# Expert 0 as a narrow block that shares the stretch of place 2; weight loads and stages in pairs

## The chip, the cores and the metric

One NeuronCore of a Trainium2 chip runs the whole kernel. The metric is the device time of one execution in microseconds. The kernel before was timed in three runs, and one more execution was profiled.

## The reference, cut to what matters

The kernel computes a two-layer decoder trunk on 256 tokens of 1024 features in fp32: a recurrent mixer and a dense SwiGLU, then a differential attention and a mixture of eight experts, of which each token takes two. The change lies in the mixture of experts:

```python
logits = xt @ w_router                       # 256 tokens x 8 experts
top_v, top_e = lax.top_k(logits, 2)
gates = softmax(top_v)
# per expert e, for the tokens x that chose it:
gu = x @ w13[e]                              # 1024 -> 2 * 3584
y  = (silu(gu[:, :3584]) * gu[:, 3584:]) @ w2[e]
out[token] += gate * y
```

Each expert's weights are 3 x 1024 x 3584 fp32 numbers, 44 MB. With the reference's inputs the experts 0 to 7 are chosen by 36, 21, 66, 43, 130, 105, 85 and 26 tokens.

## The kernel before, in words

**Numbers as pairs.** Every fp32 operand is split in a high part of type fp32r (ScalarE copies it) and a low remainder (VectorE subtracts). A product is then three matmuls on TensorE: high x high, low x high, high x low (`mm3`, lines 306 to 309). Tokens are the stationary operand (128 x 128), weights the moving one (128 x 512).

**Stream** (lines 35 to 89) brings the weights: `load` issues 1 MB loads on SyncE's queue as long as a slot is free, `split` makes a set of each half of a load (ScalarE line 77, VectorE line 78) as long as one of five pairs of parts is free, and `take` hands a set to TensorE. So the split runs at most five sets ahead of TensorE. Slots are four `raw`, the two `x_hi` and `x_lo`, `h1` (`h` in the profile), four `early` ones (`e`) and, once each, `h3_hi` and `h3_lo`. The `early` slots go round until `retire` takes them back in expert 3, where a pool named `mt` gets their memory.

**Places and blocks.** Expert 0 is at place 0; the experts 1 to 7 are sorted by their number of tokens, and take the places 1 to 7. `plan` works the order, the ranks and the gates out on VectorE and GpSimd, step by step beside the first sets. A place has blocks of 128 tokens (wide) or 64 (narrow). Place 1 has a wide and a narrow block, 0 and 2 to 4 have a wide one, 5 to 7 a narrow one. In a wide block a set costs six matmuls of 512 columns. A narrow block holds the high parts of its tokens in 64 columns of the stationary operand and the low parts in the other 64, so a set costs four (lines 1186 and 1187), and the two halves of the result are added by four small matmuls with `fold`, two stacked unit matrices (line 1207), where a wide block has four transposes (line 1197).

**Stages.** A place has seven chunks of 512 hidden columns; each has a stage g (gate half), u (other half) and w (back to 1024 features), of four sets each. `stages` orders them g0 u0 g1 u1 w0 g2 u2 w1 and so on. `moe_seq` is 0, then 2, then 3, then place 1 with the narrow places 7, 6, 5 mixed in by `merge`, then 4. After each set `beat_` takes a step of `quick` (the sums or transposes of the last chunk) and at every second set one of `slow` (plan, gathers, results). If more tokens than a place holds chose an expert, a branch behind the stages (`more`) would run another block.

Of the kernel before, what the change touches and what calls it, by code (L numbers as in the profile page):

```python
# [19 lines left out]
T = 256  # L20
D = 1024
# [13 lines left out]
class Stream:  # L35


    def __init__(self, nc, free, room):

        self.nc, self.free, self.room = nc, deque(free), deque(room)  # L40
        self.todo, self.loaded, self.ready, self.hold, self.retired = deque(), deque(), deque(), False, ()

    def add(self, ap, a, b, cols=False):
        self.todo.append((ap, a, b, cols))

    def add_plain(self, dst, src):

        self.todo.append((src, dst, None, None))

    def load(self):  # L50
        while self.todo and (self.todo[0][2] is None or self.free):
            ap, a, b, cols = self.todo.popleft()
            if b is None:
                self.nc.sync.dma_start(a, ap)
                continue
# [37 lines left out]
def trunk(ctx, tc, x, mem, a_w_in, a_conv_w, a_conv_b, a_w_rgate, a_b_rgate, a_w_igate, a_b_igate,  # L93
# [56 lines left out]
    PLACE = {0: [(0, 0, 128)], 1: [(1, 0, 128), (1, 128, 64)], 5: [(5, 0, 64)], 6: [(6, 0, 64)], 7: [(7, 0, 64)]}  # L150
# [4 lines left out]
    def stages(p):  # L155
        for j in range(NJ + 1):
            if j < NJ:
                yield (p, "g", j)
                yield (p, "u", j)
            if j:  # L160
                yield (p, "w", j - 1)

    def chain(*places):

        out_ = []
        for p in places:
            s_ = list(stages(p))
            out_ = out_[:-1] + s_[:2] + out_[-1:] + s_[2:] if out_ else s_
        return out_
# [17 lines left out]
    assert moe_seq[-5] == (4, "w", NJ - 3)  # L187
    moe_seq.insert(-2, moe_seq.pop(-5))
# [8 lines left out]
    def stage_loads(seq):  # L197
        def rows_(w, p, r0, nk, c0, n):
            if p == 0:
                return wslice(w[0, 0], r0, nk, c0, n)  # L200
            return lambda: w[0, ds(expert_id(p), 1), r0:r0 + nk * 128, c0:c0 + n].rearrange(
                "o (k p) f -> p (o k) f", p=128)

        for p, kind, j in seq:
            for k in range(2):
                if (p, kind, j, k) == (4, "w", NJ - 1, 1):

                    for r in range(2):
                        yield rows_(moe_w2, p, j * 512 + k * 256 + r * 128, 1, 0, D), 1, D
                elif kind == "w":  # L210
                    yield rows_(moe_w2, p, j * 512 + k * 256, 2, 0, D), 2, D
                else:
                    yield rows_(moe_w13, p, k * 512, 4, j * 512 + (FFN if kind == "u" else 0), 512), 4, 512
# [707 lines left out]
    for item in stage_loads(moe_seq):  # L921
        st.add(*item)
# [37 lines left out]
    def mt():  # L960

        if "mt" not in late:
            assert not any(slot in early for _, slot in st.loaded) and not any(slot in early for slot in st.free)
# [8 lines left out]
    early = [(rp, f"e{i}", True) for i in range(N_EARLY)]  # L972
# [38 lines left out]
    GROUP = ([(0, 0, 128)], [(1, 0, 128)], [(1, 128, 64), (7, 0, 64)], [(6, 0, 64), (5, 0, 64)],  # L1011
# [10 lines left out]
    dispatch((0, 0, 128), val)  # L1022
# [3 lines left out]
    fold = mo.tile([128, 64], F32, name="fold")  # L1026
    y = h3
# [3 lines left out]
    def plan():  # L1031
# [25 lines left out]
        POOL.tensor_copy(ord_i, ordr[0:1])  # L1057
        yield
# [43 lines left out]
        POOL.tensor_add(fold, ident[:, 0:64], ident[:, 64:128])  # L1102
# [10 lines left out]
    class Block:  # L1113
        def __init__(self, b):
# [3 lines left out]
            self.bank = int(self.place in (5, 6, 7))  # L1118
            self.h, self.ready = {}, False

# [10 lines left out]
    def beat_():  # L1131
        beat[0] += 1
        step(quick)
        if beat[0] % 2:
            step(slow)

    def gather_first(b):

        b.x = [mw.tile([128, KT, 128], F32R, name=f"xg_{s}") for s in ("hi", "lo")]
        for k0, n in ((0, 2), (2, 2), (4, 4)):  # L1140
            p = bank()[:, :n * 128].rearrange("p (k c) -> p k c", k=n)
            for k in range(n):
# [45 lines left out]

    def hidden(b, j):

        yield
        if b.wide:
            yield
            yield
            p = bank().rearrange("p (i c) -> p i c", i=4)
            for i in range(4):
                PE.transpose(p[:, i], b.sg[:, i * 128:(i + 1) * 128], ident)  # L1197
            hd = [mt().tile([128, 4, 128], F32R, name="hs", bufs=4) if (b.place, j) == (4, NJ - 1) else
                  mw.tile([128, 4, 128], F32R, name=f"hd_{s}") for s in ("hi", "lo")]
            hi, lo = hd  # L1200
        else:
            h = mt().tile([128, 4, 64], F32, name="sh")
            for src in (b.gs, b.us):

                p = bank()[:, :256].rearrange("p (i c) -> p i c", i=4)
# [267 lines left out]
```

## Time and profile before

| | us |
|---|---|
| median of 3 runs | 1606.11 |
| lowest and highest | 1605.93, 1607.49 |
| the profiled execution | 1606.54 |
| its span, from first to last instruction | 1604.8 |
| TensorE busy | 1582.8 (99%) |
| VectorE busy | 1263.1 (79%) |
| ScalarE busy | 1091.9 (68%) |

The span misses 1.7 us of the execution's time. The mixture of experts begins at 572 us with the first sets of expert 0, and its last stage ends at 1588 us. A busy share is an average over the whole span; the matmuls' ends are modelled, so two matmuls that follow each other overlap in the records, and their price is read from start to start.

### The profile page before, as it was taken

How to read it: one execution, taken by the hardware profiler on the slowest of the kernel's cores; microseconds unless marked ns; L12 is line 12 of the kernel's file. 1: busy time of each engine (PE TensorE's matmuls, PEld its weight loads, DVE VectorE, ACT ScalarE, POOL GpSimd, SP SyncE). 2: the span in 40 equal slices, each digit the busy share in tenths (PEclk: the TensorE clock that was granted, in tenths of full speed). 3: DMA queues.
4: the chain of work that ended last, by engine and by line, in shares of the span. 5: the costliest groups of instructions: out<-in, count | busy, mean ns of one | idle time of the engine just before them, and what ended most of it. 6: DMA issues, size and time to landing. Idle time of an engine off the chain costs nothing.

```text
span 1604.8 us, 23215 instructions
## 1 busy us (share of the span) xinstructions
PE 1582.8 (99%) x8585; PEld 1340.6 (84%) x8585; DVE 1263.1 (79%) x1464; ACT 1091.9 (68%) x1419; POOL 37.1 (2%) x60
## 2 busy tenths in 40 slices
PE   8999999999999999999999999999999999999996
PEld 7988999998998877888888888888888888888775
DVE  6678545546657689888988879888798889789976
ACT  5784544443546368787787778778778777778774
POOL 0000000000000113000000000000000000000000
PEclk9999999999999999999999999999999999999998
DMA  9454655556443789999996999999999999999991
GB/s 290 158 190 151 237 185 185 184 187 205 135 133 135 272 302 352 356 357 332 360 364 224 352 309 341 355 357 370 326 354 359 362 365 345 336 362 359 342 321 47
DMA packets 218682, 451.63 MB, mean 281 GB/s; under 512 B 7241, under 2 KB 62610, under 8 KB 218562
## 3 DMA queue, kind: packets, MB, share of 16 engines
q1 hardware_dynamic: 217490, 446.76, 78.5%
q0 software_dynamic: 1072, 3.32, 0.7%
q8 instruction: 69, 1.13, 0.3%
q14 instruction: 51, 0.42, 0.1%
HBM read 449.00 MB, written 1.05 MB: 280 GB/s over the span
## 4 chain that ended last, share of the span: by engine, by line
PE 93%; DVE 3%; ACT 2%; issue 1%; DMA 1%; POOL 0%; POOLq 0%; SPq 0%; ACTq 0%
PE mm L307 14%; PE mm L309 14%; PE mm L308 14%; PE mm L1186 7%; PE mm L1187 7%; PE acc L307 7%; PE acc L308 7%; PE acc L309 7%; PE mm L1207 3%; PE acc L1186 3%; PE acc L1187 2%; DVE w_lo L78 2%; PE mm L1170 1%; PE mm L1197 1%; ACT w_hi L77 1%
## 5 line engine op out<-in xcount | busy, mean ns | idle before, releaser
L78 DVE TENSOR_TENSOR w_lo<-raw,w_hi 128x1024 fp32r<-128x1024 f32 x509 | 610.1, 1223 | 188.3 <-ACT w_hi L77 184.8
L77 ACT ACTIVATE w_hi<-raw 128x1024 fp32r<-128x1024 f32 x509 | 525.3, 1056 | 141.4 <-PE mm L308 42.8
L307 PE MATMUL mm<-w_hi,xg_hi 128*128 128x512 f32 x560 | 225.2, 402 | 0.2 <-ACT w_hi L77 0.2
L307 PE MATMUL mm<-x_hi,w_hi 128*128 128x256 f32 x768 | 220.4, 287 | 2.4 <-ACT w_hi L77 2.4
L308 PE MATMUL mm<-w_lo,xg_hi 128*128 128x512 f32 x560 | 221.4, 395 | 1.2 <-DVE w_lo L78 1.2
L309 PE MATMUL mm<-w_hi,xg_lo 128*128 128x512 f32 x560 | 221.3, 395 | 0.0
L309 PE MATMUL mm<-x_hi,w_lo 128*128 128x256 f32 x768 | 218.6, 285 | 1.1 <-DVE w_lo L78 1.1
L308 PE MATMUL mm<-x_lo,w_hi 128*128 128x256 f32 x768 | 218.0, 284 | 0.0
L1186 PE MATMUL mm<-w_hi,xs 128*128 128x512 f32 x448 | 179.0, 400 | 0.0
L1187 PE MATMUL mm<-w_lo,xs 128*128 128x512 f32 x448 | 176.9, 395 | 0.0
L307 PEld LDWEIGHTS mm<-x_hi,w_hi 128*128 128x128 f32 x768 | 148.0, 193 | 5.6 <-ACT w_hi L77 2.9
L309 PEld LDWEIGHTS mm<-x_hi,w_lo 128*128 128x128 f32 x768 | 148.0, 193 | 1.7 <-DVE w_lo L78 1.6
L308 PEld LDWEIGHTS mm<-x_lo,w_hi 128*128 128x128 f32 x768 | 148.0, 193 | 0.6
L307 PEld LDWEIGHTS mm<-w_hi,xg_hi 128*128 128x128 f32 x560 | 105.3, 188 | 25.7 <-ACT xs L1352 1.5
L309 PEld LDWEIGHTS mm<-w_hi,xg_lo 128*128 128x128 f32 x560 | 105.1, 188 | 25.2
L308 PEld LDWEIGHTS mm<-w_lo,xg_hi 128*128 128x128 f32 x560 | 105.4, 188 | 24.9 <-DVE w_lo L78 2.2
L78 DVE TENSOR_TENSOR w_lo<-x_hi,w_hi 128x1024 fp32r<-128x1024 f32 x86 | 103.7, 1223 | 15.3 <-ACT w_hi L77 15.2
L78 DVE TENSOR_TENSOR w_lo<-x_lo,w_hi 128x1024 fp32r<-128x1024 f32 x86 | 103.4, 1222 | 13.4 <-ACT w_hi L77 13.2
L78 DVE TENSOR_TENSOR w_lo<-h,w_hi 128x1024 fp32r<-128x1024 f32 x84 | 100.9, 1222 | 14.4 <-ACT w_hi L77 14.0
L307 PE MATMUL acc<-w_hi,hd_hi 128*128 128x512 f32 x272 | 108.1, 398 | 0.0
L308 PE MATMUL acc<-w_lo,hd_hi 128*128 128x512 f32 x272 | 107.4, 395 | 0.0
L309 PE MATMUL acc<-w_hi,hd_lo 128*128 128x512 f32 x272 | 107.4, 395 | 0.0
(379 smaller groups left out, 2645.6 us busy)
## 6 DMA issues: line engine op xcount, KB each, us to landing
raw<-in_moe_w SPq DMA_DIRECT2D x169, 1024.0 KB, 5.5
x_hi<-in_moe_w SPq DMA_DIRECT2D x43, 1024.0 KB, 5.4
x_lo<-in_moe_w SPq DMA_DIRECT2D x43, 1024.0 KB, 6.2
raw<-in_ffn_w SPq DMA_DIRECT2D x42, 1024.0 KB, 5.0
h<-in_moe_w SPq DMA_DIRECT2D x42, 1024.0 KB, 5.5
e<-in_moe_w SPq DMA_DIRECT2D x36, 1024.0 KB, 5.9
raw<-in_a_w_in SPq DMA_DIRECT2D x10, 1024.0 KB, 9.5
raw<-in_mem_w_kv SPq DMA_DIRECT2D x8, 1024.0 KB
```

Of the source, the lines that this page charges most:

```text
L77: nc.scalar.activation(hi, src, AF.Copy)
L78: nc.vector.tensor_sub(lo, src, hi.bitcast(F32))
L307: PE.matmul(o, lhsT=l_hi, rhs=r_hi, start=start, stop=False)
L308: PE.matmul(o, lhsT=l_hi, rhs=r_lo, start=False, stop=False)
L309: PE.matmul(o, lhsT=l_lo, rhs=r_hi, start=False, stop=stop)
L1170: PE.matmul(p[:, k], lhsT=src[:, t, f], rhs=disp[:, t, g0:g0 + ng], start=t == 0, stop=t == 1)
L1186: PE.matmul(o[h], lhsT=w[:, kt], rhs=w_hi[:, i, f], start=a, stop=False)
L1187: PE.matmul(o[h], lhsT=w[:, kt], rhs=w_lo[:, i, f], start=False, stop=z)
L1197: PE.transpose(p[:, i], b.sg[:, i * 128:(i + 1) * 128], ident)
L1207: PE.matmul(p[:, i], lhsT=src[:, i * 128:(i + 1) * 128], rhs=fold, start=True, stop=True)
```

## The change

**Places.** Expert 0 becomes a narrow block of 64 tokens. It runs its first four runs alone (`head`), the rest is mixed by `merge` with place 2, which starts at its ninth stage.

**Stages in pairs.** `stages` now gives lists of two stages: g0 g1, u0 u1, g2 g3, w0 w1, u2 u3, and so on; `merge` and `join` move such runs as a whole.

**Loads.** For a pair of g or u stages four loads of 2 x 128 rows and 1024 columns (4 KB pieces of a row instead of 2 KB) come together: the first halves of all four feed the first stage, the second halves the second, so each of the four slots is held until the second stage is split. A load for w takes two neighbouring rows per partition (8 KB instead of 2 x 4 KB); so that the sums still meet, `rows_of` takes every second hidden column when the chunk is transposed or folded. The `early` slots are used once. The first loads of other experts wait in `Stream.load` until `plan` has made the order known (`known`).

**Sums.** `turn_half` folds the g half and the u half apart, each three sets behind its copy out of the accumulator. While the head runs, `slow` steps at every set, and the gather of place 2 follows `plan` at once. The rows of the last norm (`late_rows`) use other buffers, and the branch for too many tokens covers more cases.

```diff
-    PLACE = {0: [(0, 0, 128)], 1: [(1, 0, 128), (1, 128, 64)], ...
+    PLACE = {0: [(0, 0, 64)], 1: [(1, 0, 128), (1, 128, 64)], ...
     def stages(p):
-        for j in range(NJ + 1):
-            if j < NJ:
-                yield (p, "g", j)
-                yield (p, "u", j)
-            if j:
-                yield (p, "w", j - 1)
+        runs = [range(j, min(j + 2, NJ)) for j in range(0, NJ, 2)]
+        for n, js in enumerate(runs):
+            yield [(p, "g", j) for j in js]
+            if n:
+                yield [(p, "w", j) for j in runs[n - 1]]
+            yield [(p, "u", j) for j in js]
+        yield [(p, "w", j) for j in runs[-1]]
...
-        return a[:-1] + b[:2] + a[-1:] + b[2:]
-    moe_seq = join(chain(0, 2, 3), merge(chain(1), chain(7, 6, 5)))
+        return a[:-1] + b[:1] + a[-1:] + b[1:]
+    head = 4
+    moe_seq = chain(0)[:head] + merge(chain(2), chain(0)[head:])
+    moe_seq = join(join(moe_seq, chain(3)), merge(chain(1), chain(7, 6, 5)))
...
+    def add_all(self, loads, cols=False):
+        loads = [(self.n + i, *load, cols) for i, load in enumerate(loads)]
+        self.n += len(loads)
+        self.todo += loads
+        for h in range(2 if loads[0][2] > 1 else 1):
+            self.cuts += [(load[0], h) for load in loads]
...
     def load(self):
-        while self.todo and (self.todo[0][2] is None or self.free):
+        while self.todo and (self.todo[0][0] is None or self.free):
+            if callable(self.todo[0][1]) and not self.known:
+                return
...
     def split(self):
-            halves, slot = self.loaded[0]
-            src = halves.pop(0)
-            if not halves:
-                self.loaded.popleft()
-                if slot[2] and slot not in self.retired:
+            n, h = self.cuts.popleft()
+            halves, slot = self.loaded[n]
+            src = halves[h]
+            if h == len(halves) - 1:
+                del self.loaded[n]
+                if slot[2]:
                     self.free.append(slot)
...
             if kind == "w":
+                        a = rows_(moe_w2, p, j * 512 + k * 256, 2, 0, D, "(p k)")
...
+                if len(run) == 2:
+                    yield [(rows_(moe_w13, p, k * 256, 2, c0, 1024), 2, 1024) for k in range(4)], True
...
-    early = [(rp, f"e{i}", True) for i in range(N_EARLY)]
+    early = [(rp, f"e{i}", False) for i in range(N_EARLY)]
...
-        if beat[0] % 2:
+        if beat[0] % 2 or beat[0] < 8 * head:
             step(slow)
...
+    def rows_of(a, i):
+        n = i // 2 * 256 + i % 2
+        return a[:, n:n + 255:2]
+
+    def turn_half(b, j, a, u):
+        yield
+        yield
+        yield
+        p = bank()[:, :256].rearrange("p (i c) -> p i c", i=4)
+        for i in range(4):
+            PE.matmul(p[:, i], lhsT=rows_of(a, i), rhs=fold, start=True, stop=True)
+        if not u:
+            b.sh[j] = b.room([128, 4, 64], F32, "sh")
+            ACT.activation(b.sh[j], p, AF.Silu)
+            return
+        h = b.sh.pop(j)
+        DVE.tensor_mul(h, h, p)
+        yield
+        hd = b.room([128, 4, 128], F32R, "hs")
+        hi, lo = hd[:, :, 0:64], hd[:, :, 64:]
+        ACT.activation(hi, h, AF.Copy)
+        DVE.tensor_sub(lo, h, hi.bitcast(F32))
+        b.h[j] = hd
...
-        (0, "u", 3): [ask(4, True, blocks[2])],
-        (3, "g", 2): [retire],
...
-    slow.append(plan())
+    slow += [plan(), gather(4, True, blocks[2])]
```

On TensorE, the first products behind expert 0's gather. Before, each weight row block takes three matmuls on the wide block `xg`:

```order
L307 MATMUL mm<-w_hi,xg_hi 128x512
L308 MATMUL mm<-w_lo,xg_hi 128x512
L309 MATMUL mm<-w_hi,xg_lo 128x512
L307 MATMUL mm<-w_hi,xg_hi 128x512
L308 MATMUL mm<-w_lo,xg_hi 128x512
L309 MATMUL mm<-w_hi,xg_lo 128x512
```

and now two on the narrow block, which lies in the buffer `ys`:

```order
L1231 MATMUL mm<-w_hi,ys_5635 128x512
L1232 MATMUL mm<-w_lo,ys_5635 128x512
L1231 MATMUL mm<-w_hi,ys_5635 128x512
L1232 MATMUL mm<-w_lo,ys_5635 128x512
```

One set is the six rows of the first and the four of the second piece.

On VectorE, the plan's steps for the gates among the splits of expert 0's weights (`w_lo`). The reduction to `gate` reads products that GpSimd makes from the result of the reciprocal. Before:

```order
L1072 RECIPROCAL g_5939<-g_5939 128x2
L78 TENSOR_TENSOR w_lo<-e_5590,w_hi 128x1024
L1216 TENSOR_TENSOR hd_lo<-mm,hd_hi 128x512
L78 TENSOR_TENSOR w_lo<-e_5592,w_hi 128x1024 x2
L78 TENSOR_TENSOR w_lo<-x_hi,w_hi 128x1024
L1083 TENSOR_REDUCE gate<-tmp 128x2x7
L78 TENSOR_TENSOR w_lo<-x_hi,w_hi 128x1024
L78 TENSOR_TENSOR w_lo<-x_lo,w_hi 128x1024
L1088 TENSOR_REDUCE cs<-cmp 128x7
```

and now:

```order
L1108 RECIPROCAL g_5820<-g_5820 128x2
L95 TENSOR_TENSOR w_lo<-h_hi,w_hi 128x1024
L95 TENSOR_TENSOR w_lo<-h_lo,w_hi 128x1024
L1119 TENSOR_REDUCE gate<-tmp 128x2x7
L95 TENSOR_TENSOR w_lo<-h_5584,w_hi 128x1024
L1124 TENSOR_REDUCE cs<-cmp 128x7
L95 TENSOR_TENSOR w_lo<-e_5586,w_hi 128x1024
L1131 TENSOR_REDUCE over<-cs 128x1
```

Between the reciprocal and the reduction stood four splits and a remainder; now two splits stand there.

On SyncE, the queue of loads where the static ones of expert 0 end. Before (the rows before these are the first twelve loads of the mixture):

```order
L59 DMA e_5592<-in_moe_w 128x4x512
L59 DMA x_hi<-in_moe_w 128x4x512
L59 DMA x_lo<-in_moe_w 128x2x1024
L59 DMA raw<-in_moe_w 128x2x1024
```

and now, at the same place, with the read of the experts' order (`TENSOR_LOAD`) behind 16 loads:

```order
L71 DMA e_5592<-in_moe_w 128x2048
L71 DMA x_hi<-in_moe_w 128x2048
L71 DMA x_lo<-in_moe_w 128x2048
L71 DMA raw<-in_moe_w 128x2048
L213 TENSOR_LOAD ord_i
L71 ISA
L71 DMA raw<-in_moe_w 128x2x1024
```

The 16 loads before the read feed the head; place 2's first load stands right behind it, and its pieces are twice as long.

## Rows read from the trace of the kernel before

**Rows 1.** The page: busy time, share of the span and instructions of each engine; and the chain that ended last, by engine.
```profile
PE 1582.8 (99%) x8585; PEld 1340.6 (84%) x8585; DVE 1263.1 (79%) x1464; ACT 1091.9 (68%) x1419; POOL 37.1 (2%) x60
PE 93%; DVE 3%; ACT 2%; issue 1%; DMA 1%; POOL 0%; POOLq 0%; SPq 0%; ACTq 0%
```

**Rows 2.** The longest waits of TensorE's matmuls (PE) and of its weight loads (PEld) from 572 to 1588 us: who waited for whom, us in total, times, longest.
```profile
PE mm L308 <- DVE w_lo L78: 1.2, 2, 0.8
PEld mm L308 <- DVE w_lo L78: 2.2, 3, 1.1
```

**Rows 3.** Three windows: length, then busy us and number of instructions of PE, PEld, DVE, ACT and POOL, the granted TensorE clock, the share of the transfer engines and GB/s.
```profile
600.00:860.00 260.00, 259.56 (x1184) 210.83 (x1183) 234.57 (x230) 206.23 (x233) 12.25 (x21) 1.00 0.98 353
1020.00:1140.00 120.00, 120.00 (x592) 99.66 (x592) 104.52 (x104) 94.26 (x118) 0.00 (x0) 1.00 1.00 363
1400.00:1520.00 120.00, 120.00 (x567) 97.62 (x567) 113.79 (x118) 95.52 (x114) 2.09 (x4) 1.00 0.98 355
```

**Rows 4.** Timeline of TensorE: start, length, instruction, number of records. The first row is expert 0's first matmul, that of 819.59 expert 3's first. From 660.02 to 665.62 there are 24 matmuls from start to start. L1170 are gather products, L1197 transposes, L1207 folds (four of them in eight records).
```profile
572.41 0.48 PE L307 MATMUL mm<-w_hi,xg_hi 128*128 128x512 f32 x1
...
630.47 0.39 PE L309 MATMUL mm<-w_hi,xg_lo 128*128 128x512 f32 x1
630.70 0.56 PE L1170 MATMUL mm<-disp,h_hi 128*128 128x128 f32 x4
...
631.38 0.39 PE L308 MATMUL mm<-w_lo,xg_hi 128*128 128x512 f32 x1
...
660.02 0.40 PE L309 MATMUL mm<-w_hi,xg_lo 128*128 128x512 f32 x1
...
665.62 0.40 PE L309 MATMUL mm<-w_hi,xg_lo 128*128 128x512 f32 x1
...
709.89 0.40 PE L309 MATMUL acc<-w_hi,hd_lo 128*128 128x512 f32 x1
710.12 0.60 PE L1197 MATMUL mm<-ident,sg 128*128 128x128 f32 x4
...
710.79 0.39 PE L308 MATMUL mm<-w_lo,xg_hi 128*128 128x512 f32 x1
...
819.59 0.48 PE L307 MATMUL mm<-w_hi,xg_hi 128*128 128x512 f32 x1
...
1280.07 0.39 PE L1187 MATMUL acc<-w_lo,hs 128*128 128x512 f32 x1
1280.30 1.00 PE L1207 MATMUL mm<-fold,gs 128*128 128x64 f32 x8
...
1281.43 0.40 PE L1187 MATMUL acc<-w_lo,hs 128*128 128x512 f32 x1
```

**Rows 5.** Timeline of VectorE from expert 0's first sets on; in brackets idle time before the instruction and what ended it. The split at 574.27 is the first after the gather, the one at 616.36 the 31st.
```profile
574.27 1.23 DVE L78 TENSOR_TENSOR w_lo<-x_hi,w_hi 128x1024 fp32r<-128x1024 f32 x1 [0.25 <-ACT w_hi L77]
...
588.01 0.68 DVE L1303 TENSOR_TENSOR sg<-sg,mm 128x512 f32<-128x512 f32 x1
...
594.03 0.68 DVE L1216 TENSOR_TENSOR hd_lo<-mm,hd_hi 128x512 fp32r<-128x512 f32 x1
...
605.33 0.15 DVE L1072 RECIPROCAL g<-g 128x2 f32<-128x2 f32 x1
605.41 1.21 DVE L78 TENSOR_TENSOR w_lo<-e,w_hi 128x1024 fp32r<-128x1024 f32 x1
606.53 0.68 DVE L1216 TENSOR_TENSOR hd_lo<-mm,hd_hi 128x512 fp32r<-128x512 f32 x1
607.13 2.35 DVE L78 TENSOR_TENSOR w_lo<-e,w_hi 128x1024 fp32r<-128x1024 f32 x2
609.40 1.22 DVE L78 TENSOR_TENSOR w_lo<-x_hi,w_hi 128x1024 fp32r<-128x1024 f32 x1
611.43 0.26 DVE L1083 TENSOR_REDUCE gate<-tmp 128x14 f32<-128x98 f32 x1 [0.81 <-POOL tmp L1082]
...
616.36 1.21 DVE L78 TENSOR_TENSOR w_lo<-raw,w_hi 128x1024 fp32r<-128x1024 f32 x1
...
621.63 1.22 DVE L1107 TENSOR_TENSOR h_lo<-h,h_hi 128x1024 fp32r<-128x1024 f32 x1
...
630.17 4.62 DVE L78 TENSOR_TENSOR w_lo<-e,w_hi 128x1024 fp32r<-128x1024 f32 x4
```

**Rows 6.** Groups of instructions by line: the product and the remainder of a narrow block's hidden columns on VectorE; busy us in total, mean ns of one, idle time before.
```profile
L1216 DVE TENSOR_TENSOR hs<-sh,hs 128x256 fp32r<-128x256 f32 x28 | 11.8, 421 | 0.0
L1211 DVE TENSOR_TENSOR sh<-sh,mm 128x256 f32<-128x256 f32 x28 | 11.7, 416 | 0.0
```

**Rows 7.** Timeline of GpSimd (POOL) between that reciprocal and that reduction.
```profile
605.57 1.09 POOL L1073 TENSOR_TENSOR d<-d,g 128x2 f32<-128x2 f32 x1 [15.66 <-DVE g L1072]
...
607.08 3.61 POOL L1078 TENSOR_TENSOR ge<-ge,c 128x16 f32<-128x16 f32 x1
...
610.89 0.50 POOL L1082 TENSOR_TENSOR tmp<-sel,ge 128x49 f32<-128x49 f32 x2
```

**Rows 8.** SyncE's transfer queue in two windows, first from 180 to 430 us, then from 600 to 860 us: packets, MB, and the time that they took as a share of 16 engines' time.
```profile
q1 hardware_dynamic: 33995, 45.36, 54.2%
...
q1 hardware_dynamic: 38388, 91.50, 98.0%
```

**Rows 9.** The page: transfers by slot and tensor, number, KB each, median us from issue to landing.
```profile
raw<-in_moe_w SPq DMA_DIRECT2D x169, 1024.0 KB, 5.5
```

More of the change, by code (lines that the diff above doesn't have):

```diff
@@ L166, in chain @@
         for p in places:
[L167 to L168 removed]
+            out_ = join(out_, list(stages(p)))
         return out_
@@ L962, in mt @@
         if "mt" not in late:
-            assert not any(slot in early for _, slot in st.loaded) and not any(slot in early for slot in st.free)
+            assert not st.uses(early)
             ep.close()
@@ L1117, in __init__, with room @@
             self.wide = self.n == 128
-            self.bank = int(self.place in (5, 6, 7))
+            self.bank = int(self.place in (0, 5, 6, 7))
             self.h, self.ready = {}, False
+            self.sg, self.sh = {}, {}
+        def room(self, shape, dtype, name):
+            if "mt" in late or not st.uses(early):
+                pool, bufs = mt(), {"xs": 3, "gu": 3, "sh": 4, "hs": 4}[name]
+            else:
+                pool, bufs = mw, 2
+                name = {"xs": "ys0", "gu": "sg", "sh": "hd_hi", "hs": "hd_lo"}[name]
+            return pool.tile(shape, dtype, name=name, bufs=1 if name == "ys0" else bufs)
     quick, slow, beat = deque(), deque(), [0]
@@ L1189, in hidden @@
     def hidden(b, j):
         yield
[L1192 to L1205, printed above, removed]
-                for i in range(4):
-                    PE.matmul(p[:, i], lhsT=src[:, i * 128:(i + 1) * 128], rhs=fold, start=True, stop=True)
-                if src is b.gs:
-                    ACT.activation(h, p, AF.Silu)
-                else:
-                    DVE.tensor_mul(h, h, p)
-                yield
-            hd = mt().tile([128, 4, 128], F32R, name="hs", bufs=4)
-            hi, lo, p = hd[:, :, 0:64], hd[:, :, 64:], h
+        yield
@@ L1215, in hidden @@
+        yield
+        p = bank().rearrange("p (i c) -> p i c", i=4)
+        for i in range(4):
+            PE.transpose(p[:, i], rows_of(b.sg[j], i), ident)
+        del b.sg[j]
+        hd = [mt().tile([128, 4, 128], F32R, name="hs", bufs=4) if (b.place, j) == (4, NJ - 1) else
+              mw.tile([128, 4, 128], F32R, name=f"hd_{s}") for s in ("hi", "lo")]
+        hi, lo = hd
         ACT.activation(hi, p, AF.Copy)
@@ L1347, in spread @@
             gb.extend(mt().tile([128, D], F32, name="xs", bufs=3) for _ in range(2))
[L1348 removed]
+            for i in range(4):
                 p = bank()
[L1350 removed]
+                f = slice(i % 2 * 512, (i % 2 + 1) * 512)
+                PE.matmul(p, lhsT=slots[0:1, 1:2].to_broadcast([1, 128]), rhs=rows[i // 2][:, f], start=True, stop=True)
                 yield
[L1352 removed]
+                ACT.activation(gb[i // 2][:, f], p, AF.Copy)
         slow.append(spread())
[L1356 to L1360 removed]
     hooks = {
[L1363 removed]
         (2, "g", 0): [gathered(*blocks[2])],
@@ L1386, in trunk @@
     with tc.If(more > 0):
-        for p in (0, 1, 2, 3, 5, 6, 7):
+        rooms = {p: sum(b[2] for b in bs) for p, bs in PLACE.items()}
+        most = {p: T if p < 2 else 2 * T // p for p in PLACE}
+        for p, base in ((p, base) for p in PLACE for base in range(rooms[p], most[p], 128)):
             c = nc.values_load(cs_i[0:1, p:p + 1], min_val=0, max_val=2 * T,
                                skip_runtime_bounds_check_because="a count of at most 256 tokens")
-            with tc.If(c > 0):
-                key = (p, sum(b[2] for b in PLACE[p]), 128)
+            with tc.If(c > base - rooms[p]):
+                key = (p, base, 128)
                 where[key] = (0, 0)
@@ L1400, in trunk @@
                 s2 = stream()
+                s2.known = True
                 for item in stage_loads(seq):
-                    s2.add(*item)
-                for p_, kind, j in seq:
-                    run_stage([b], kind, j, s2)
+                    s2.add_all(*item)
+                for run in seq:
+                    for _, kind, j in run:
+                        run_stage([b], kind, j, s2)
                 wait_slow()
     fs = [slice(h * 512, (h + 1) * 512) for h in range(2)]
-    ys = [mt().tile([128, 512], F32, name=n) for n in ("gs", "us")]
+    ys = [mt().tile([128, 512], F32, name="gu", bufs=3) for _ in range(2)]
     ACT.activation(ys[0], last.acc[0], AF.Copy)
```

114 lines of the change are left out of this document (57 added, 57 removed).

## The prediction

> **What bounds the kernel now.** I read the page first: TensorE (PE) is busy for 99% of the span and makes up 93% of the chain that ended last [rows 1]. A busy PE can still be a waiting PE, so the waits come next: between 572 and 1588 us, the whole mixture of experts, PE waited 1.2 us for the low half of a weight and its weight loads 2.2 us for the same thing [rows 2]. The windows show how little the others have left: from 600 to 860 us VectorE (DVE) is busy for 234.6 of 260 us and the transfers for 0.98 of the time; both stay near there to the end [rows 3]. So three resources are nearly full, and PE is the one that sets the end. The timeline gives its prices [rows 4]: 24 matmuls of 512 columns start within 665.62 - 660.02 = 5.60 us, 0.2333 us each, with the granted clock at 1.00 throughout, the 2.4 GHz level [rows 3]. A set (half a load) is 6 of them for a wide block, 1.40 us, and 4 for a narrow one, 0.93 us. DVE splits a set in (4.62 - 1.22)/3 = 1.135 us when sets follow each other [rows 5]: less than a wide set, more than a narrow one.
>
> **Expert 0 narrow: PE's work.** Expert 0 has 7 x 12 = 84 sets. Two matmuls less in each are 168 x 0.2333 = 39.2 us. What comes in: per 512 hidden columns two groups of four sums by fold in place of one group of four transposes. From 1280.07 to 1281.43 us there are two ordinary matmuls and one group of folds: 1.36 - 0.47 = 0.89 us; from 709.89 to 710.79 the same with transposes: 0.90 - 0.47 = 0.43 us [rows 4]. So 7 x (1.79 - 0.43) = 9.5 us come back. Net **-29.7 us**. The first gather keeps its 16 products; I cost their halved width at nothing.
>
> **The head, 32 sets of expert 0 alone.** Here PE no longer sets the pace. Its work is 32 x 0.933 + four groups of folds 3.6 + the gather for place 2, eight groups of 630.70's kind (0.91 - 0.47 = 0.44 us each), 3.5: together 37.0 us. DVE's work I take from its own timeline [rows 5]. In the kernel before, 31 splits after the gather and the plan's steps in between end at 617.5 us (616.36 + 1.135). The change takes out two wide products and two hidden remainders, 2 x (0.68 + 0.68) = 2.7 us. It puts in four narrow steps of 0.42 us [rows 6], 1.7 us, and, since the plan now steps at every set, the two remainders of the layer's rows before the 32nd set: 2 x 1.22 = 2.4 us. And DVE's wait for GpSimd grows: from the product at 605.57 to the end of the second product at 610.89 + 0.50 GpSimd needs 5.8 us [rows 7]. Before, four splits and a remainder stood between DVE's reciprocal and the reduction that reads the result, and 0.81 us were waited; now two splits stand there (2.3 us), so 3.5 are waited: +2.7. The 32nd split ends at 617.5 - 2.7 + 1.7 + 2.4 + 2.7 = 621.6 us, PE's set a narrow set later, at 622.5. From 572.4 that is 50.1 us for 37.0 us of work: PE stands 13.1 us, 1.2 of which it stood before. **+11.9 us.** GpSimd's shorter steps (the products ahead of the order and the ranks) could add 0 to 2 us more; as their covers are about as long as they are, I take 0.
>
> **From the ninth stage to expert 3.** Before, expert 3 begins at 819.59 us, 247.2 us after expert 0 [rows 4]. PE's work there is now 247.2 - 1.2 - 29.7 = 216.3, less the head's 37.0: 179.3 us, so expert 3 begins at 801.8. Does anything else need longer? DVE: 132 splits of 1.135 = 150 us and some 16 us of products: covered, since wide sets let it get its five sets ahead again. Transfers: by the queue's rows, 45.36 MB in 33,995 packets took 0.542 x 250 = 135.5 us, and 91.50 MB in 38,388 packets 0.980 x 260 = 254.8 us [rows 8]. Two equations for 16 engines give 9.8 ns a packet and 40.4 us a MB: a load (1.0486 MB) took 2.91 us with the old mean of 427 packets and is estimated at 2.78 with 213. The early slots are now used once and seven slots go round; four are held until the second stage of a pair is split, so load 23 goes out with the 37th split, at 621.6 + 5 x 1.135 = 627.3 us. The 60 loads up to expert 3's first then end at 627.3 + 60 x 2.78 = 794, and two splitting steps later, at 796, PE could begin: 6 us early, hidden. With 2.91 they would end at 802 + 2: 2 us late. So this term is 0 to 2; I take 0, since the packets' price comes from this trace. The rows show a queue that moved 359 GB/s while it was busy [rows 8], with 2 and 4 KB packets.
> The Trainium skill has a rule against this term ("DMA: Bandwidth & Descriptors", Where 436 GB/s comes from): between HBM and SBUF a core's share of HBM, about 358 GB/s, is the bound. By it, larger packets win nothing, a load stays at an estimated 2.93 us, the term is 3 us and the time 1592. The trace speaks against it as a ceiling: from 1020 to 1140 us the mean was 363 GB/s [rows 3].
>
> **After that** PE's count is unchanged. The narrow sums stand three sets behind their copy, before one set; PE did not wait for them before, so nothing is gained. The runs of two stages make bursts: between two runs of expert 1 there are now 24 narrow sets in place of 12. PE needs 24 x 0.933 + 4 x 0.89 = 26.0 us for them, DVE 24 x 1.135 + 4 x 0.42 = 28.9: 2.9 us that the five sets in stock (5.7 us of DVE's work) must cover. I cost it at 0, with 2.9 x 12 bursts = 35 us as the other end. The weights' columns are now read with a step of two where they are summed or transposed. No row shows such a read: between nothing and a doubling of a weight load. The folds' records start 0.11 us apart (eight in 0.89), so a doubling is +0.11 on 35 x 16 + 28 x 4 = 672 records, +74 us. I take 0, as all contiguous groups in the rows cost the same 0.11 whatever they load. The Trainium skill ("SBUF — State Buffer", Door 1: The DMA port swizzle) says that fp32 can be read with a step of up to four at no price; no run here shows it. Late loads of the last norm's rows, the shifted fold and the longer branch that isn't entered lie beside PE: 0 (36 of the reference's tokens choose expert 0, so its 64 places suffice and the branch stays closed).
>
> **Sum.** 1606.5 (the profiled execution) - 29.7 + 11.9 = 1588.7; the median of the runs is 0.4 lower, so about **1588.5 us**.
>
> **Rivals.**
> (a) The head isn't bound by DVE: then all of PE's saving shows, and its old wait goes: 1606.1 - 29.7 - 1.2 = 1575. For it: DVE's steps overlap a little more than their sum. Against: in the kernel before DVE is already without a gap from 574 to 639 us [rows 5] and PE only just keeps up with it. 8%.
> (b) Part of it is eaten: GpSimd's waits 2, larger packets that move no faster 2 (60 x 2.91), and 6 to 11 us in bursts: 1598 to 1603. For it: from 600 to 860 us the transfers were at 0.98 of their time [rows 3]. Against: each has a cover in the sums above. 11%. The Trainium skill's rule above is the case of the packets.
> (c) **Slower:** the bursts of 24 narrow sets are bound by the splits, since DVE waits for ScalarE's half and ScalarE for PE's sums, so that the stock of five is not full when a burst begins. Place: expert 1 with 7, 6 and 5. Price up to 35 us: 1588.5 + 35 = 1623. It decides from 17.6/12 = 1.5 us a burst. For it: DVE is already at 104.5 of 120 us there [rows 3]. Against: 15 us of 120 are left over. 9%.
> (d) **Slower:** with seven slots of which four are held, the queue runs dry. A load lands 5.5 us after its issue [rows 9], 2.7 more than it streams; once for each of the 21 pairs of gate or up stages where one wide block sets the pace: 57 us, 1645; from 0.8 us a pair on there is no gain left. Against: 8 wide sets take 11.2 us and their four loads 11.1, so each load has some three sets of time to spare. 6%.
> (e) **Slower:** the step of two doubles the weight loads: 1588.5 + 74 = 1662. 3%.
>
> **Numbers.** Forecast 1581 to 1597 with 55%; the rest (8%) is that several of these cancel the gain, and about 0.2% (3 us) is what a measurement of this kernel can tell from no change. Faster 55 + 8 + 11, and one from the rest: 0.75; same 0.07; slower 9 + 6 + 3: 0.18. The range 1577 to 1606 leaves out the slower cases and little of (a).
>
> **What would show it.** Between PE's first narrow set and the first wide set about 50 us, with PE's gaps put down to DVE's w_lo and one DVE wait of 3 to 4 us for GpSimd's tmp; from there to expert 3 no PE wait over 2 us and a start near 802; as many us from there to the end as before; a transfer rate over 370 GB/s where the queue is full. The forecast is wrong if PE waits for DMA-fed splits between 650 and 800 us, if DVE's waits return once per burst after 940 us, or if fold groups take more than 0.9 us.

## The result and the profile after

The changed kernel takes **1618.03 us** (median of 4 runs, 1615.52 to 1619.89), against 1606.3 before: a ratio of **1.0071, 95% interval 1.0053 to 1.0088**. The forecast was 1588.5 us. The profiled execution took 1616.94 us, its span is 1615.2, 10.4 more than before. Busy times and chain of the page after, the rows that answer to [rows 1]:

```profile
PE 1579.5 (98%) x8505; PEld 1319.3 (82%) x8505; DVE 1255.3 (78%) x1464; ACT 1088.7 (67%) x1433; POOL 29.5 (2%) x58
PE 86%; DVE 5%; ACT 4%; DMA 2%; issue 2%; POOL 0%; SPq 0%; POOLq 0%; ACTq 0%; DVEq 0%
```

PE has 80 records less, but 7% of the chain has gone from PE, 4 of them to DVE and ScalarE (ACT). Where, the first matmuls of each stretch tell. Timeline of PE after: expert 0's first narrow set, place 2's first wide set, expert 3, expert 1, place 4.

```profile
572.85 0.48 PE L1231 MATMUL mm<-w_hi,ys 128*128 128x512 f32 x1
...
627.67 0.39 PE L341 MATMUL mm<-w_hi,xg_hi 128*128 128x512 f32 x1
...
807.17 0.48 PE L341 MATMUL mm<-w_hi,xg_hi 128*128 128x512 f32 x1
...
937.97 0.40 PE L341 MATMUL mm<-w_hi,xg_hi 128*128 128x512 f32 x1
...
1460.73 0.40 PE L341 MATMUL mm<-w_hi,xg_hi 128*128 128x512 f32 x1
```

The same for expert 1 and place 4 before (expert 0 and expert 3 stand in [rows 4]):

```profile
949.74 0.48 PE L307 MATMUL mm<-w_hi,xg_hi 128*128 128x512 f32 x1
...
1451.64 0.39 PE L307 MATMUL mm<-w_hi,xg_hi 128*128 128x512 f32 x1
```

| stretch, us | before | forecast | after |
|---|---|---|---|
| head: first narrow set to place 2 | - | 50.1 | 54.8 |
| from there to expert 3 | - | 179.3 | 179.5 |
| both: expert 0 to expert 3 | 247.2 | 229.4 | 234.3 |
| expert 3 | 130.2 | 130.2 | 130.8 |
| expert 1 with 7, 6, 5 | 501.9 | 501.9 | 522.8 |
| place 4 to the end | 153.2 | 153.2 | 154.5 |

So 12.9 us are won up to expert 3 and 20.9 lost in the stretch of expert 1 (0.4, 0.6 and 1.3 lie in the start, in expert 3 and at the end). What PE waits for in the whole mixture, as in [rows 2] (matmuls, then weight loads; us, times, longest):

```profile
PE mm L1232 <- DVE w_lo L95: 6.9, 16, 0.8
PE mm L1215 <- ACT xg_hi L1219: 3.2, 1, 3.2
...
PEld mm L1232 <- DVE w_lo L95: 33.3, 70, 1.1
```

L1232 is the narrow product with the low part: 33.3 us of weight loads that wait for a split, 2.2 us before. 12.1 of them lie in the head, 21.2 in the stretch of expert 1. Of the 12 bursts of narrow sets there, five have 24 sets, six have 20 and the last 12. Two windows (columns as in [rows 3]), first while expert 1's sets go through its wide and its narrow block, then a burst of 24 narrow sets:

```profile
996.20:1014.90 18.70, 18.70 (x86) 15.26 (x86) 12.93 (x13) 11.68 (x15) 0.00 (x0) 1.00 0.99 384
1014.90:1046.10 31.20, 30.61 (x149) 23.49 (x147) 29.50 (x33) 25.46 (x33) 0.00 (x0) 1.00 0.83 307
```

DVE is busy for 69% of the first and 95% of the second. Its timeline shows why that doesn't balance, with ScalarE's row and the burst's first matmul in between:

```profile
1008.52 1.23 DVE L95 TENSOR_TENSOR w_lo<-x_hi,w_hi 128x1024 fp32r<-128x1024 f32 x1 [2.38 <-ACT w_hi L94]
...
1014.59 1.22 DVE L95 TENSOR_TENSOR w_lo<-x_lo,w_hi 128x1024 fp32r<-128x1024 f32 x1 [1.11 <-ACT w_hi L94]
...
1016.25 0.48 PE L1231 MATMUL acc<-w_hi,hs 128*128 128x512 f32 x1
1016.53 0.60 ACT L1272 ACTIVATE hd_hi<-mm 128x512 fp32r<-128x512 f32 x1 [1.97 <-PE mm L1267]
1017.16 0.69 DVE L1273 TENSOR_TENSOR hd_lo<-mm,hd_hi 128x512 fp32r<-128x512 f32 x1 [1.35 <-ACT hd_hi L1272]
1017.77 0.68 DVE L1359 TENSOR_TENSOR sg<-sg,mm 128x512 f32<-128x512 f32 x1
1018.60 3.50 DVE L95 TENSOR_TENSOR w_lo<-raw,w_hi 128x1024 fp32r<-128x1024 f32 x3
...
1035.70 3.49 DVE L95 TENSOR_TENSOR w_lo<-raw,w_hi 128x1024 fp32r<-128x1024 f32 x3
1039.10 0.41 DVE L1252 TENSOR_TENSOR sh<-sh,mm 128x256 f32<-128x256 f32 x1
1039.43 1.22 DVE L95 TENSOR_TENSOR w_lo<-x_lo,w_hi 128x1024 fp32r<-128x1024 f32 x1
```

Ahead of the burst it idles: 2.38 us while ScalarE stands at a Silu of folds, then 1.11 us before each split with its stock full. At the burst's first matmul (1016.25) the splits of four sets have ended, that of the set which PE begins among them (counted by order, splits against sets), and the next begins 2.35 us later: ScalarE waits for PE's transposes, DVE for ScalarE, and the wide block's remainder and product come first. In 11 of the 12 bursts four sets are ready, and 1.1 to 2.6 us pass until the next split begins. From 1018.60 on DVE has one gap in this burst, of 0.21 us, and PE comes to wait for the splits. What DVE can't store it can't make up.

**The head.** ScalarE stands for 4.0 us before the copy of the hidden columns, since DVE's product before it is behind the splits, and its copies for place 2's gather queue up:

```profile
603.69 0.42 ACT L1256 ACTIVATE hd_lo<-hd_hi 128x256 fp32r<-128x256 f32 x1 [4.04 <-DVE hd_hi L1252]
...
609.70 0.37 ACT L1219 ACTIVATE xg_hi<-mm 128x256 fp32r<-128x256 f32 x1
```

PE's next gather group waits for that copy; behind the gap the matmuls are 0.43 us apart in place of 0.23:

```profile
606.55 0.40 PE L1232 MATMUL mm<-w_lo,ys 128*128 128x512 f32 x1
610.12 1.12 PE L1215 MATMUL mm<-disp,h_lo 128*128 128x128 f32 x4 [3.17 <-ACT xg_hi L1219]
611.03 0.73 PE L1231 MATMUL mm<-w_hi,ys 128*128 128x512 f32 x1
611.57 0.63 PE L1232 MATMUL mm<-w_lo,ys 128*128 128x512 f32 x1
611.99 0.63 PE L1231 MATMUL mm<-w_hi,ys 128*128 128x512 f32 x1
```

In the windows the granted clock is 0.77 and 0.69 there, a stretch at 1.2 GHz:

```profile
606.00:610.00 4.00, 0.95 (x3) 0.47 (x3) 3.83 (x5) 4.00 (x7) 0.00 (x0) 0.77 0.72 247
610.00:618.00 8.00, 7.88 (x37) 7.00 (x38) 6.24 (x7) 6.06 (x11) 0.00 (x0) 0.69 0.02 8
```

### The profile page after: what moved, and what is told of

It is laid out like the page before. It is cut to its first block, busy times and chain, and to the rows that moved or that the text cites. A ratio compares the mean times of both kernels' runs of the same rounds, so it can differ in the third digit from the quotient of the medians.

```text
span 1615.2 us, 23099 instructions
## 1 busy us (share of the span) xinstructions
PE 1579.5 (98%) x8505; PEld 1319.3 (82%) x8505; DVE 1255.3 (78%) x1464; ACT 1088.7 (67%) x1433; POOL 29.5 (2%) x58
## 4 chain that ended last, share of the span: by engine, by line
PE 86%; DVE 5%; ACT 4%; DMA 2%; issue 2%; POOL 0%; SPq 0%; POOLq 0%; ACTq 0%; DVEq 0%
PE mm L341 13%; PE mm L343 12%; PE mm L342 12%; PE mm L1232 7%; PE mm L1231 7%; PE acc L341 6%; PE acc L342 6%; PE acc L343 6%; DVE w_lo L95 4%; PE mm L1246 3%; PE acc L1231 2%; PE acc L1232 2%; ACT w_hi L94 2%; DMA raw<-in_a_w_in 2%; PE mm L1215 1%
## 5 line engine op out<-in xcount | busy, mean ns | idle before, releaser
L95 DVE TENSOR_TENSOR w_lo<-raw,w_hi 128x1024 fp32r<-128x1024 f32 x545 | 652.2, 1221 | 212.8 <-ACT w_hi L94 211.0
L94 ACT ACTIVATE w_hi<-raw 128x1024 fp32r<-128x1024 f32 x545 | 561.8, 1058 | 144.1 <-PE mm L342 42.8
L1232 PE MATMUL mm<-w_lo,xs 128*128 128x512 f32 x448 | 181.9, 406 | 2.3 <-DVE w_lo L95 2.0
L341 PE MATMUL mm<-w_hi,xg_hi 128*128 128x512 f32 x448 | 180.8, 404 | 0.0
L342 PE MATMUL mm<-w_lo,xg_hi 128*128 128x512 f32 x448 | 177.3, 396 | 0.4 <-DVE w_lo L95 0.2
L343 PE MATMUL mm<-w_hi,xg_lo 128*128 128x512 f32 x448 | 176.9, 395 | 0.0
L1232 PEld LDWEIGHTS mm<-w_lo,xs 128*128 128x128 f32 x448 | 84.1, 188 | 38.2 <-DVE w_lo L95 21.2
L94 ACT ACTIVATE w_hi<-x_lo 128x1024 fp32r<-128x1024 f32 x95 | 99.8, 1057 | 18.5 <-DVE w_lo L95 5.4
L94 ACT ACTIVATE w_hi<-x_hi 128x1024 fp32r<-128x1024 f32 x95 | 99.8, 1056 | 11.1 <-PE acc L343 5.7
L94 ACT ACTIVATE w_hi<-h 128x1024 fp32r<-128x1024 f32 x94 | 97.9, 1056 | 7.2 <-PE mm L343 2.4
L341 PEld LDWEIGHTS mm<-w_hi,xg_hi 128*128 128x128 f32 x448 | 84.2, 188 | 21.4 <-issue 2.8
```

The lines of the kernel that those rows point to most:

```text
L94: nc.scalar.activation(hi, src, AF.Copy)
L95: nc.vector.tensor_sub(lo, src, hi.bitcast(F32))
L341: PE.matmul(o, lhsT=l_hi, rhs=r_hi, start=start, stop=False)
L342: PE.matmul(o, lhsT=l_hi, rhs=r_lo, start=False, stop=False)
L343: PE.matmul(o, lhsT=l_lo, rhs=r_hi, start=False, stop=stop)
L1232: PE.matmul(o[h], lhsT=w[:, kt], rhs=w_lo[:, i, f], start=False, stop=z)
```

## Experiments

Theory A: the bursts of 24 narrow sets outrun DVE, and the stock covers little. Rivals: the sums three sets behind, the reads with a step of two, the larger loads. The first two kernels change the length of a burst: to 12, which also takes these places' loads back to 512 columns, and to 48 (in fact 32 to 48), which changes nothing else.

**single_stretch**, 12 sets:

```diff
     def stages(p):
+        if p in (1, 5, 6, 7):      # g0 u0 g1 u1 w0 ..., each a run of its own
+            for j in range(NJ + 1): ...
+            return
```

> The changed kernel, but places 1, 7, 6 and 5 go by single stages (g0 u0 g1 u1 w0 ...), with loads of 512 columns: between two stages of place 1 stand 12 narrow sets in place of 24. Places 0, 2, 3, 4 keep their pairs. Theory A (bursts of 24 sets outrun VectorE): PE's waits for w_lo in the stretch of expert 1 go back to what they were before, the stretch falls from 522.5 to 503 to 506 us, and the time from 1618 to 1599 to 1603. Rival B (the sums three sets behind, or the reads with a step of two): nothing changes, 1616 to 1620. Rival C (pieces of 2 KB bring the queue to its limit): the splits wait for transfers instead, 1606 to 1612.

1601.43 us (ratio to before 0.9967, 0.9954 to 0.9979), 16.6 us less; the stretch takes 508.8, still above A's 503 to 506. The longest of the weight loads' waits in it:

```profile
PEld mm L1240 <- DVE w_lo L95: 1.9, 6, 0.5
```

**burst48**, 48 sets:

```diff
-            k = (n + 1) * len(b) // len(a)
+            k = (n + 1) // 2 * 2 * len(b) // len(a)
```

> The changed kernel, with 48 narrow sets between every two runs of place 1 in the stretch of expert 1, in place of 24 after each run: half as many bursts, twice as long. Theory A: VectorE needs 2.9 us more than PE per 24 sets, the stock covers about 1.1 us once per burst (24 sets lose some 1.8 us now), so 48 lose 4.7 and six bursts 28 us in place of 21: the stretch 528 to 532 us, the time 1623 to 1628. Rival B (waits that belong to each sum, not to the length of a burst): 1616 to 1620.

1629.89 us (one run). The stretch takes 536.0; time and stretch are above A's 1623 to 1628 and 528 to 532:

```profile
PEld mm L1232 <- DVE w_lo L95: 25.6, 53, 1.1
PEld acc L1232 <- DVE w_lo L95: 8.9, 26, 0.9
```

508.8, 522.8, 536.0 us with up to 12, 24, 48: the loss grows with the burst, though there are fewer of them. **parts4** takes away one set of stock:

```diff
-N_PARTS = 5
+N_PARTS = 4
```

> The changed kernel with four pairs of parts in place of five, so the split runs at most four sets ahead. Only the stretch of expert 1 is read (the phases before it suffer in ways that nobody disputes). Theory A (the stock of split sets is what a burst lives on): one split, 1.135 us, less of cover in each of 12 bursts of 24 sets: the stretch takes 533 to 537 us in place of 522.5, with PE's waits for w_lo up by as much. Rival (the cover isn't the stock, but the wide sets between bursts): 521 to 525 us.

The stretch takes 537.6 us (953.66 to 1491.25), 14.8 more, 1.2 a burst over the 12, about one split; the whole kernel takes 1649.42 (one run). The two waits above are 42.9 and 9.1 us there. In 11 of its bursts three sets are ready at the first matmul in place of four, and the next split begins as late as before. A stands.

**no_step** undoes the step of two in the pairs' kernel:

```diff
-        n = i // 2 * 256 + i % 2
-        return a[:, n:n + 255:2]
+        return a[:, i * 128:(i + 1) * 128]
```

> The changed kernel, with the loads for w as before (2 x 4 KB rows) and contiguous columns in folds and transposes in place of a step of two. If the step is what made a record of a fold 117 in place of 111 ns and one of a transpose 116 in place of 108 ns, both go back, and PE's work in the whole mixture falls by about 4 us: 1612 to 1616. If the longer records have another cause they stay, 1616 to 1620. PE's waits in the bursts stay as they are in both.

The records went back (from start to start, medians 117 to 111 ns for folds and 117 to 109 for transposes), but the time is 1617.4 us (one run), above the 1612 to 1616 expected and within the spread of the changed kernel's runs. It is measured again below.

**late_scale** and **mended** go at the head. In late_scale the copies `y` (L1145) leave the plan and stand behind the gather:

```diff
-    slow += [plan(), gather(4, True, blocks[2])]
+    slow += [plan(), gather(4, True, blocks[2]), scale_y()]
```

> The changed kernel, with ScalarE's two scaled copies of the layer's rows (1.05 us each, the last steps of the plan) moved behind the gather of place 2. Theory H1 (ScalarE's backlog behind its 4.0 us wait makes PE's gap of 3.2 us in the head, and the fall of the clock follows the gap): the gap falls to 1.3 us, the granted clock stays at 1.00 behind it, place 2's first wide set starts at 622 to 624 in place of 627.7 and the time falls by 3 to 5 us to 1613 to 1615. Rival H2 (VectorE sets the head's end and fills the gap in any case): the gap goes, but the first wide set stays at 626 to 628, the time at 1616 to 1619.

1619.17 us (ratio 1.0075, 1.0058 to 1.0092): nothing won. PE's gap is 3.4 us, now for the cast of the layer's rows (`h_hi`), which stands behind the same wait of ScalarE. **mended** is single_stretch with that, no step, and two more `yield` ahead of the copy:

> Single stages in the stretch of expert 1, contiguous columns in folds and transposes (loads for w as before), ScalarE's scaled copies behind the gather of place 2, and its copy of a narrow block's hidden columns two sets later. The contiguous columns should give back 3 to 4 us of the 1601.4. Theory H3 (in the head ScalarE waits 4.0 us at that copy for VectorE's product, the gather's copies queue behind it, PE stops for 3.3 us, and the clock falls): with the copy later the wait falls to under 2 us, PE's gap to under 1.5 us, place 2's first wide set starts at 622 to 624 in place of 626.6, and the time is 1593 to 1596. Rival H2 (VectorE's queue sets the head's end anyway): the first wide set stays at 625.5 to 627, the time 1597 to 1599.

1600.67 us (0.996, 0.9945 to 0.9974). ScalarE's wait is gone (0.3 us), but PE stands 1.8 and 1.9 us for DVE's own remainder of the rows (`h_lo`), and the first wide set stays at 627.4. H3 falls: with this order the gather comes when DVE is behind, whoever is asked first. The time is above H2's range too.

**single_all** takes the pairs away from places 0, 2, 3 and 4 too (the condition in the first diff becomes true for all, the head eight runs):

> The changed kernel with single stages and loads of 512 columns at every place; the head is 32 sets as before it (g0 u0 g1 u1 w0 g2 u2 w1), the narrow sums, the two-row loads for w and expert 0 as changed. Theory P (the longer pieces of the pairs are hidden by PE from 628 us on): the time of the kernel with single stages in expert 1's stretch alone, 1600 to 1603. Rival Q (without them the splits wait for transfers between 628 and 807 us): by 2.91 in place of 2.78 us a load 2 us later at the least, 1604 to 1612, with PE waits for DMA-fed splits there.

**1594.78 us** (0.9924, 0.9907 to 0.9941), 6.6 less than single_stretch, and better than either theory said: the pairs cost outside the bursts as well. Its timeline:

```profile
573.01 0.77 PE L1239 MATMUL mm<-w_hi,ys 128*128 128x512 f32 x1
...
623.97 0.48 PE L349 MATMUL mm<-w_hi,xg_hi 128*128 128x512 f32 x1
...
800.73 0.40 PE L349 MATMUL mm<-w_hi,xg_hi 128*128 128x512 f32 x1
```

The head takes 51.0 us in place of 54.8, with the clock at 1.00 from 580 us on. From there to expert 3 it is 176.8 in place of 179.5: with pairs place 2's last w stage stood right behind its own transposes. In the changed kernel:

```profile
797.91 0.63 PE L1267 MATMUL mm<-ident,sg 128*128 128x128 f32 x4
799.22 0.51 PE L341 MATMUL acc<-w_hi,hd_hi 128*128 128x512 f32 x1 [0.69 <-ACT hd_hi L1272]
799.56 0.39 PE L342 MATMUL acc<-w_lo,hd_hi 128*128 128x512 f32 x1
801.08 0.50 PE L343 MATMUL acc<-w_hi,hd_lo 128*128 128x512 f32 x1 [1.12 <-DVE hd_lo L1273]
```

In single_all narrow sets lie between the two, and the wait isn't there. **wide_zero** has single stages and expert 0 wide, with 0, 2, 3 in a row:

> The kernel with single stages everywhere, with expert 0 as a wide block again, and 0, 2, 3 one after the other: all that is left of the change are the two-row loads for w with their step of two, the sums three sets behind, the early slots used once and the plan at every set of the head. Theory N (expert 0 narrow is worth what the traces show up to expert 3, 247.2 us before, 228.7 with single stages, 18.5 us; the rest costs 5 to 7 us): 1611 to 1614. Rival (the rest costs nothing, and expert 0 narrow is worth only the 12 us of the net difference): 1605 to 1608.

1616.95 us (1.0062, 1.0046 to 1.0079): 22.2 us above single_all. Expert 0 narrow, mixed with place 2, is worth more than N said, and what else is left of the change costs 10 us against the kernel before, where N said 5 to 7.

**single_contig** is single_all without the step of two and the two-row loads for w that need it, **single_one** has the narrow sums one set behind as well:

> The kernel with single stages everywhere (1594.8), now with contiguous columns in folds and transposes and loads for w of 2 x 4 KB rows, as before the change. Theory S (a read with a step of two costs 5 to 6 ns more a record of a fold, 7 of a transpose): 560 and 112 records, 3 to 4 us: 1590.5 to 1592.5. Rival (pieces of 4 KB in place of 8 KB slow the loads, which are near their limit from 680 to 800 us): the gain is lost there, 1594 to 1598.

> The kernel before it in this call, with the narrow sums one set behind their copy, as before the change, in place of three. With single stages the stretch of expert 1 still takes 507 us, before the change 502: 2.4 of the 5 are the step of two. Theory D (sums three sets behind put VectorE's products and remainders into the wrong place of a burst of 12): the stretch falls to 502 to 503 us and the time by 2 to 3 us below the kernel before it, to 1588 to 1590. Rival (the place of the sums is indifferent): within 1 us of it.

1591.72 us (0.9906, 0.989 to 0.9923): the step costs 3.1 us, as theory S said. And 1595.58 us (0.993, 0.9913 to 0.9946): theory D falls the wrong way round, three sets behind are 3.9 us better than one. Its stretch takes 508.3 us, that of single_contig 505.7.

**late_silu** and **late_both** follow ScalarE's waits:

```diff
         if not u:
+            yield
+            yield
             b.sh[j] = b.room([128, 4, 64], F32, "sh")
             ACT.activation(b.sh[j], p, AF.Silu)
```

> Single stages everywhere and contiguous columns (1591.7), with ScalarE's Silu of a narrow g half two sets behind its fold in place of right behind it. In that kernel the stretch of expert 1 still takes 505.7 us where it was 501.9 before the change, and ScalarE stands 47 us there before this Silu, since it runs some sets ahead of PE. Theory E (that wait holds up the splits queued behind it on ScalarE, and PE's waits at the next burst come from it): ScalarE's wait falls below 20 us, the stretch to 502 to 503.5 us, the time to 1588.5 to 1590.5. Rival (ScalarE has the time to spare): within 1 us of 1591.7.

> The kernel before it, with ScalarE's copy of the narrow hidden columns (hs) one set later as well; ScalarE stands 38 us before that copy for VectorE's product. Theory E would give another 0.5 to 1.5 us in the stretch and a shorter head; the rival (time to spare) nothing, and a loss of 0.5 to 1 us where a w stage then waits for the later copy.

1591.0 us (0.9902, 0.9885 to 0.9918) and 1592.03 (0.9908, 0.9891 to 0.9924): as times, the rival's. But in late_silu the stretch takes 502.1 us, as before the change, PE waits for no split in it any more, and ScalarE's 47 us before the Silu are gone: theory E holds there. (late_both has the same stretch, 502.1, and gains nothing.) In the head PE now waits 3.8 us in one place (5.2 in late_both), and the clock falls:

```profile
601.95 0.80 PE L1239 MATMUL acc<-w_hi,hd_lo 128*128 128x512 f32 x1 [3.80 <-DVE hd_lo L1266]
```

```profile
600.00:608.00 8.00, 6.05 (x18) 5.18 (x19) 8.00 (x13) 7.66 (x10) 3.29 (x3) 0.60 0.41 133
```

**late_silu_1** puts `if b.place:` ahead of the two yields, so expert 0 keeps the early Silu:

> Single stages, contiguous columns, and the later Silu for every narrow block but expert 0's, so the head has its old order. Theory F (in the head the order of ScalarE's steps makes PE's gap, after which the granted clock falls, and costs 1 to 3 us; in the stretch of expert 1 the later Silu gives 3.7): no stretch of low clock between 580 and 1570 us, place 2's first wide set 55.6 us behind the first gather as with the early Silu, the stretch at 502 us, the time 1587.5 to 1589.5. Rival (head and clock vary from run to run, whatever the order): 1590.5 to 1592.

**1587.53 us** (0.988, 0.9863 to 0.9896), the fastest here. The clock stays up in the head, which takes 624.01 - 573.19 = 50.8 us, and the stretch takes 502.0:

```profile
600.00:608.00 8.00, 7.48 (x37) 5.49 (x37) 7.90 (x12) 7.61 (x10) 3.29 (x3) 1.00 0.41 131
```

```profile
573.19 0.48 PE L1239 MATMUL mm<-w_hi,ys 128*128 128x512 f32 x1
...
624.01 0.48 PE L349 MATMUL mm<-w_hi,xg_hi 128*128 128x512 f32 x1
...
931.04 0.48 PE L349 MATMUL mm<-w_hi,xg_hi 128*128 128x512 f32 x1
...
1433.07 0.48 PE L349 MATMUL mm<-w_hi,xg_hi 128*128 128x512 f32 x1
```

## Why the prediction was wrong, step by step

**The step that failed** is "I cost it at 0, with 2.9 x 12 bursts = 35 us as the other end". The deficit of 2.9 us came from the right rows, but it holds for a burst of 24 sets, of which there are five (252 narrow sets in all, where 12 x 24 are 288); and it left out the wide block's remainders and product, which DVE makes in a burst too. The cover was too large: I took all five sets as stock (5.7 us). Four are ready when a burst begins (4.5 us), and DVE goes on splitting only 1.1 to 2.6 us later, in the burst shown because PE's transposes, ScalarE's copy and the wide block's sums come first. Some 2 to 3.5 us are left. Of the 20.9 us that the stretch lost, 13.9 come from making bursts of 12 into bursts of up to 24 sets, 1.2 a burst. parts4 shows that it is the stock: one set less costs about one split a burst. My own rival (c) named mechanism (ScalarE waits for PE's sums, DVE for ScalarE) and place, with a chance of 9%; its argument against, "15 us of 120 are left over", averaged over bursts and the idle time between them.

**The head** was the second miss: 54.8 us for 50.1. Where stages are single the DVE sum comes out: 51.0 and 50.8 us, the 32nd split ended at 621.8 in single_all, 621.6 forecast. Part of that is luck: GpSimd's wait was too dear (1.1 us there and 1.4 in the changed kernel, for 3.5), and about as much in a later start and in other waits of DVE wasn't in the sum. With pairs the gather meets the layer's casts while DVE is behind, PE stands 3.2 us and then has a stretch at 1.2 GHz. The kernels with the pairs' head have such a stretch between 603 and 618 us, late_silu and late_both one from 601 or 602 on; single_all, single_contig, single_one and late_silu_1 have none there. What of the 4 us is the clock and what the order isn't separated; but with 3.4 us at 1.2 GHz there (single_stretch, burst48, no_step) the head takes 54.1 to 54.2 us, with 6.8 us (the changed kernel, late_scale, mended) 54.3 to 54.8. And the order isn't enough: parts4, whose mixture begins 14 us later, has the pairs' head too, and takes 51.0 us with a longest gap of 1.7. One reading under rival (a) was wrong: VectorE was not without a gap from 574 to 639 us, [rows 5] have one of 0.81.

**Right in the number**: the 179.5 us from there to expert 3 (179.3 forecast), in which the missing matmuls and the folds show; but two errors cancel in it: PE's waits of some 2 us at 799 us, which I had not seen, and a miscount, since six groups of folds stand in the head (48 records), not four, so 1.8 us of PE's work fewer are left behind it. In single_all and late_silu_1 this part takes 176.8 and 176.2 us, and expert 3 starts at 800.7 and 800.2 us, where 801.8 was forecast. Expert 0 narrow is worth 22.2 us between wide_zero and single_all, where the first two terms together gave 17.8.

**The step of two** at 0 was nearly right: a group of folds between two ordinary matmuls takes 1041.20 - 1039.80 - 0.47 = 0.93 us, against 0.89 [rows 4], beyond the 0.9 named as a limit:

```profile
1039.80 0.40 PE L1232 MATMUL mm<-w_lo,xs 128*128 128x512 f32 x1
1040.04 1.04 PE L1246 MATMUL mm<-fold,gu 128*128 128x64 f32 x8
1040.89 0.48 PE L1231 MATMUL mm<-w_hi,xs 128*128 128x512 f32 x1
1041.20 0.40 PE L1232 MATMUL mm<-w_lo,xs 128*128 128x512 f32 x1
```

In single_contig it is 0.89 again, and 3.1 us come back. The Trainium skill ("SBUF — State Buffer", Door 1: The DMA port swizzle) gives a step of up to four fp32 for free; for these weight loads it is cheap, not free.

**The sums three sets behind** were said to gain nothing; against one set they gain 3.9 us once the kernel has these stages, and the Silu right behind the fold, which holds up ScalarE's splits, costs 3.7 us in the stretch. The prediction had no row for either. Rivals (d) and (e) didn't come: between 628 and 938 us no matmul waits for a split (weight loads do for 1.5 us in all), and the step costs 3 us, not 74.

**The transfers** cost nothing, as forecast, but the price was wrong. The window from 680 to 800 us after, with the longer pieces:

```profile
680.00:800.00 120.00, 119.16 (x538) 96.12 (x536) 114.06 (x107) 100.49 (x112) 0.00 (x0) 1.00 1.02 402
```

and in single_contig, with the old ones:

```profile
680.00:800.00 120.00, 120.00 (x551) 97.68 (x550) 113.92 (x109) 101.73 (x114) 0.00 (x0) 1.00 1.04 395
```

395 GB/s without any longer piece, where 353 at a share of 0.98 had looked full [rows 3]: a load in 2.65 us, where "9.8 ns a packet" gave 2.91. The same window before the change, with the same pieces but wide sets alone:

```profile
680.00:800.00 120.00, 120.00 (x548) 97.70 (x548) 106.45 (x100) 93.73 (x107) 0.00 (x0) 1.00 0.98 348
```

And wide_zero, which differs from single_all in expert 0's block and place alone, has 347 GB/s there against 395. The rate followed what PE took, and the price was read from a queue that wasn't at its limit. So the sign "over 370 GB/s" came true for another reason than the longer pieces. The rule of the Trainium skill ("DMA: Bandwidth & Descriptors", Where 436 GB/s comes from) that about 358 GB/s binds doesn't hold in these windows either.

**What adds up.** In the stretch of expert 1, 522.8 us become 508.8 without pairs there, 507.2 without any, 505.7 without the step, 502.0 with the later Silu; before it was 501.9. Over the kernel, wide_zero, single_all and the changed kernel put the parts at about +10 (the rest of the change, with single stages), -22 (expert 0 narrow) and +23 us (the pairs). Of the +10, the step and the Silu were found; some 3 us aren't separated. With the pairs and the two smaller costs taken out, the time is 1587.5. That this is near the 1588.5 forecast for the whole change is chance.

## What to carry to other kernels

Where one engine prepares for another through a small stock, compare the two by the longest run of work of one kind, not by their averages: the stock covers what is ready when the run begins, less the time until the first engine goes on making more, and idle time before it counts for nothing. Mix short and long work as finely as the loads allow. When sums are placed sets behind their input, place what the other engines do with them as far behind, or they wait in order and hold up what is queued there.

## What the runs showed of the hardware

A share of 1.0 of the transfer engines' time was no ceiling: shares of 0.98 to 1.04 went with 348 to 402 GB/s. In the head, PE gaps of 3.2 to 5.2 us (in mended two of 1.8 and 1.9 close together) went with 3.4 to 6.8 us at 1.2 GHz, matmuls of 512 columns about 0.43 us apart. Of shorter gaps some did and some didn't: after 1.1 us at 801 us burst48 has 3.4 us at 1.2 GHz, after the same 1.1 us at 800 us the changed kernel has none. What decides it stays open. A weight load of 128 fp32 columns with a step of two made a fold's record, from start to start, 117 in place of 111 ns, a transpose's 117 in place of 109.
